# Norm weights folded into the rounding of x, K tile by K tile, in a two-layer encoder trunk on one core

## The chip, the core and the metric

The kernel runs on one core of a Trainium2 chip. TensorE (PE, with its weight loads PEld), VectorE (DVE), ScalarE (ACT), GpSimd (POOL) and SyncE (SP, which issues the DMAs here) each work through a queue of their own in order, and wait for one another by semaphores. The metric is the time of one execution on the device in microseconds; less is better.

## The reference

The trunk has two layers on 256 tokens of width 1024. Each layer is a half-step feed-forward block, a mixer, and a second half-step feed-forward block, and each of the three starts with an RMS norm:

```python
def rmsnorm(x, g):
    x32 = x.astype(jnp.float32)
    y = x32 * lax.rsqrt(jnp.mean(x32 * x32, axis=-1, keepdims=True) + EPS)
    return (y * g.astype(jnp.float32)).astype(x.dtype)
...
    for i in range(DEPTH):
        h = rmsnorm(x, ffn1_norm[i])
        x = x + 0.5 * swiglu(h, ffn1_w_gate[i], ffn1_w_up[i], ffn1_w_down[i])
        h = rmsnorm(x, mix_norm[i])
        proj = h @ w_in[i]
        ...
        x = x + jnp.concatenate([o_s, o_m], axis=-1) @ w_out[i]
        h = rmsnorm(x, ffn2_norm[i])
        x = x + 0.5 * swiglu(h, ffn2_w_gate[i], ffn2_w_up[i], ffn2_w_down[i])
```

`swiglu` is `(silu(h @ w_gate) * (h @ w_up)) @ w_down` with an inner width of 2816. The mixer of layer 0 is chunked attention with a learned bias, that of layer 1 is differential attention with rotary positions; both have four heads of attention into a memory of 256 rows besides. Everything is in 32-bit floats.

## The kernel before, in words

**Products.** Every operand of a product is split into a high part, rounded to the type fp32r, and a low part, the rest. `dense` makes one product of a 128-row K tile: three matmuls into the same PSUM bank, high by high (line 379), high by low of the weights (382), low of x by high of the weights (385), each 128x128 by 128x512.

**Weights.** They come in chunks of 1 MB (`raw`, three buffers, loads in line 270), are rounded by ACT (`hi`, line 300) and DVE (`lo`, line 310) in four quarters of 512 columns, and stay in four pairs of buffers. The chunks of the first feed-forward block are cut in four loads each for the first two chunks; the loads of x are issued between them.

**x.** It lies as two blocks of 128 tokens, each in two halves of 512 columns. `prep_half` turns one half of one token block into the left operand: four transposes on PE into one PSUM bank `xtp` (line 392), a multiply with the norm weight on DVE (`y`, line 423; after the transpose the weight of a column is one value per partition), a cast on ACT (`xh`, line 426), and a subtraction on DVE (`xl`, line 428). A half holds four K tiles; x has eight (`KT`), K tiles 0 to 3 in half 0 and 4 to 7 in half 1. The factor of the row, 1/rms, is applied after the products: `square` sums the squares on ACT (line 437), `prep_rstd` makes `xr` of them.

`prep_half` runs 24 times: four times at the start (`start`), and four times at each of the five entries to the following stages, from `finish`, which adds the accumulated sum to x (lines 462 and 465) half by half.

**Order.** The order on each queue is not written out; a planner sets it while the program is built. `Flow` keeps a clock `now`, advanced by the estimated time of each matmul or transpose, and a time `free` for each other engine. Steps are generators: a `yield` of a time means "not before", a `yield` of a function means "when this holds". Whenever PE's clock moves, steps that are due are issued, those due earliest first; weight rounding (`split_hi`, `split_lo`) is spawned as idle work, issued when nothing else is due. `dense` waits until the planner has its operands: `xt.t[tb][k]` for x and `lot` for the weights. The estimates are

```python
HOP = 0.22
T_MM = 0.216
T_TR = 0.107
...
    def act(self, n, extra=0.0):
        return self.eng("A", 0.15 + n / 1200.0 + extra)
    def dve(self, n, extra=0.0):
        return self.eng("V", 0.07 + n / 960.0 + extra)
```

The start of the kernel is set by hand: the clock begins at 2.7, the four halves of x are due at four written times (line 1308: 3.75 for block 0 half 0, 8.2 for block 0 half 1, 7.4 for block 1 half 0, 10.4 for block 1 half 1), and arrivals of weights are estimated in `loader` from 2.3 on with 2.9 for a chunk and 1.5 of latency. The first feed-forward block takes K tiles 0 to 3 of both token blocks, then 4 to 7 of both.

Of the kernel before, what the change touches and what calls it, by code (L numbers as in the profile page):

```python
# [12 lines left out]
F32 = mybir.dt.float32  # L13
# [3 lines left out]
AF = mybir.ActivationFunctionType  # L17
ALU = mybir.AluOpType
AX = mybir.AxisListType

P = 128
# [121 lines left out]
def kernel(  # L143
# [10 lines left out]
    nc = tc.nc  # L154
    PSUM = bass.MemoryType.PSUM
    NRAW, NHL, NT2 = 3, 4, 19
    flow = Flow()
# [13 lines left out]
    g2 = Slots(flow, t2, "t", NT2)  # L171
# [5 lines left out]
    def bank(name, shape=(P, 4, P)):  # L177
        return banks.take(list(shape), F32, name)
# [36 lines left out]
    gcol = const.tile([P, NGC], F32, name="gcol")  # L215
    gcs = const.tile([P, 4], F32, name="gcs")

    def gain_columns():
        grow = const.tile([NGC - 16, P], F32, name="grow")
        for src, r0 in ((mix_norm, GC_MIX), (mem_norm, GC_MEM), (ffn2_norm, GC_FFN2)):  # L220
            later(grow[r0 - 16:r0, :], src.rearrange("l (k p) -> (l k) p", p=P))
        for src, r0, n in ((mem_q_norm, GC_MQ, 2), (mem_k_norm, GC_MK, 2), (a_q_norm, GC_AQ, 1),
                           (a_k_norm, GC_AK, 1)):
            for j in range(2):
                later(grow[r0 - 16:r0 - 16 + n, j * HD:(j + 1) * HD], src)
        later(grow[GC_SUB - 16:GC_SUB - 15, :], b_subln)
        yield from loaded()
        yield banks.has()
        tp = bank("gps")
        nc.tensor.transpose(out=tp[:, 0, :NGC - 16], in_=grow, identity=ident[:NGC - 16, :NGC - 16])  # L230
        yield flow.pe(T_TR)
        nc.vector.tensor_copy(gcol[:, 16:], tp[:, 0, :NGC - 16])
        banks.give()
        nc.vector.tensor_scalar_mul(gcs[:, 0:2], gcol[:, GC_MQ:GC_MQ + 2], HD ** -0.5)
        nc.vector.tensor_scalar_mul(gcs[:, 2:3], gcol[:, GC_AQ:GC_AQ + 1], HD ** -0.5)
        nc.vector.tensor_scalar_mul(gcs[:, 3:4], gcol[:, GC_SUB:GC_SUB + 1], 1.0 - LAMBDA_INIT)
        flow.dve(0, 0.5)
# [153 lines left out]
    def turn(dst, src, flipped=False):  # L391
        nc.tensor.transpose(out=dst, in_=src, identity=flip if flipped else ident)  # L392
        return flow.pe(T_TR)
# [19 lines left out]
    def prep_half(xt, tb, hf, gc, wait=0.0):  # L413
        yield banks.has()
        tp = bank("xtp")
        for k in range(4):
            t = turn(tp[:, k, :], xs[tb][:, hf * 512 + k * P:hf * 512 + (k + 1) * P])
        yield t
        yield g2.has()
        y = g2.take([P, 4, P], F32, "y")  # L420
        ks = slice(hf * 4, hf * 4 + 4)
        g = gcol[:, gc + hf * 4:gc + hf * 4 + 4]
        nc.vector.tensor_tensor(out=y, in0=tp, in1=g.unsqueeze(2).broadcast_to([P, 4, P]), op=ALU.mult)
        banks.give()
        yield flow.dve(512)
        nc.scalar.copy(out=xt.h[tb][:, ks, :], in_=y)
        yield flow.act(512)
        nc.vector.tensor_sub(xt.l[tb][:, ks, :], y, xt.h[tb].bitcast(F32)[:, ks, :])
        g2.give()
        t = flow.dve(512)  # L430
        for k in range(hf * 4, hf * 4 + 4):
            xt.t[tb][k] = t
        flow.spawn(square(xt, tb, hf, flow.now + wait))

    def square(xt, tb, hf, t):
        yield t
        nc.scalar.activation(junk, xs[tb][:, hf * 512:(hf + 1) * 512], AF.Square,
                             accum_out=xt.ss[tb][:, hf:hf + 1])
        yield flow.act(512, 0.1)
        xt.done[tb] += 1  # L440
        if xt.done[tb] == 2:
            yield from prep_rstd(xt, tb)
# [13 lines left out]
    def finish(acc, tb, xt, gc, half):  # L456
        for hf in range(2):
            sl = slice(hf * 512, (hf + 1) * 512)
            yield lambda: acc.t[tb][hf] is not None
            yield acc.t[tb][hf]  # L460
            if half:
                nc.vector.scalar_tensor_tensor(out=xs[tb][:, sl], in0=acc.ps[tb][hf], scalar=0.5, in1=xs[tb][:, sl],
                                               op0=ALU.mult, op1=ALU.add)
            else:
                nc.vector.tensor_add(xs[tb][:, sl], acc.ps[tb][hf], xs[tb][:, sl])
            banks.give()
            yield flow.dve(512)
            if xt is None:
                nc.sync.dma_start(out=out[0, tb * P:(tb + 1) * P, sl], in_=xs[tb][:, sl])
            else:  # L470
                yield from prep_half(xt, tb, hf, gc)
# [807 lines left out]
    xt = Xt()  # L1279
# [12 lines left out]
    def start(tb, hf, t):  # L1292
        yield t
        yield from prep_half(xt, tb, hf, GC_FFN1, 3.0)
# [10 lines left out]
    flow.spawn(start_gain())  # L1305
    for tb in range(2):
        for hf in range(2):
            flow.spawn(start(tb, hf, (3.75, 8.2, 7.4, 10.4)[2 * tb + hf]))
    flow.spawn(gain_columns())
    flow.spawn(rope_setup(), idle=True)  # L1310
    flow.spawn(lambda_setup())
# [2 lines left out]
    for l in range(DEPTH):  # L1314
        xt = ffn(l, 1, xt, GC_MIX + l * KT)
        xt = mixer(l, xt, GC_FFN2 + l * KT)
        xt = ffn(l, 2, xt, None if l == DEPTH - 1 else GC_FFN1 + (l + 1) * KT)
# [53 lines left out]
```

## Time and profile before

| | |
|---|---|
| median of 3 runs | 970.88 us (970.84 to 972.41) |
| the profiled execution | 970.84 us, span in the profile 969.1 us |
| busy: PE, PEld, DVE, ACT, POOL | 960.4, 788.3, 681.8, 545.7, 60.2 us |
| granted PE clock | 1.00 |
| moved by DMA | 204 MB, 211 GB/s on average |

The span is the time from the first to the last recorded event; what lies around it, 1.7 us, is not in the records. PE counts as busy while a matmul is in flight, and matmuls overlap, so its 99% does not say that it works at its peak; it says that there is hardly a stretch without one.

### The profile page before, as it was taken

To read this page: it belongs to the slowest core of one execution; us is meant where nothing else is said; L and a number is where in the kernel's file an instruction comes from. 1 tells how busy PE (TensorE), PEld (TensorE's weight loads), DVE (VectorE), ACT (ScalarE), POOL (GpSimd) and SP (SyncE) were. 2 spreads that over 40 slices of the span, in tenths; PEclk is the share of its full clock that TensorE was granted. 3 is DMA by queue.
4 is the path that set the end of the run, shared out by engine and by line. 5 is a ranking of instruction groups with operands and counts; after the bars stand their busy time and mean duration, and the time that the engine had idled before them with its cause. 6 is when DMAs were issued, how large, how long until landed. Compare 5 with 4: busy or idle time off the path is not lost.

```text
span 969.1 us, 13332 instructions
## 1 busy us (share of the span) xinstructions
PE 960.4 (99%) x4552; PEld 788.3 (81%) x4552; DVE 681.8 (70%) x1428; ACT 545.7 (56%) x1167; POOL 60.2 (6%) x65
## 2 busy tenths in 40 slices
PE   8999999999999999999999999999999999999998
PEld 7888888888777888888888888888787788888886
DVE  6777777788787877665566666654999986666641
ACT  6665555667675655554455545443677764545440
POOL 0000000021210000000000000000344100000000
PEclk9999999999999999999999999999999999999999
DMA  9988877385525587776648777764641468877741
GB/s 286 323 272 279 262 261 242 128 283 195 175 90 171 182 254 238 237 248 231 197 132 275 245 228 247 239 218 132 211 137 50 139 199 265 252 249 240 236 131 43
DMA packets 169295, 204.03 MB, mean 211 GB/s; under 512 B 9674, under 2 KB 144395, under 8 KB 169227
## 3 DMA queue, kind: packets, MB, share of 16 engines
q1 hardware_dynamic: 169226, 203.18, 65.3%
q8 instruction: 35, 0.57, 0.2%
q14 instruction: 34, 0.27, 0.1%
HBM read 188.99 MB, written 14.16 MB: 210 GB/s over the span
## 4 chain that ended last, share of the span: by engine, by line
PE 93%; DVE 4%; ACT 1%; DMA 1%; SPq 0%; issue 0%; ACTq 0%
PE gu L385 16%; PE gu L382 16%; PE gu L379 16%; PE acc L379 10%; PE acc L385 10%; PE acc L382 10%; PE pj L385 3%; PE pj L382 3%; PE pj L379 3%; DVE lo L310 1%; PE xtp L392 1%; PE S L1012 1%; PE AV L1093 1%; PE ptp L392 1%; PE kv L382 1%; PE kv L385 1%
## 5 line engine op out<-in xcount | busy, mean ns | idle before, releaser
L310 DVE TENSOR_TENSOR lo<-raw,hi 128x512 fp32r<-128x512 f32 x656 | 418.0, 684 | 196.2 <-ACT hi L300 182.6
L300 ACT CAST hi<-raw 128x512 fp32r<-128x512 f32 x656 | 367.0, 618 | 281.0 <-PE gu L385 149.9
L385 PE MATMUL gu<-hi,xl 128*128 128x512 f32 x704 | 274.3, 390 | 0.0
L379 PE MATMUL gu<-hi,xh 128*128 128x512 f32 x704 | 274.1, 389 | 0.0
L382 PE MATMUL gu<-lo,xh 128*128 128x512 f32 x704 | 274.0, 389 | 0.0
L382 PEld LDWEIGHTS gu<-lo,xh 128*128 128x128 f32 x704 | 132.2, 188 | 27.4
L385 PEld LDWEIGHTS gu<-hi,xl 128*128 128x128 f32 x704 | 132.2, 188 | 27.3
L379 PEld LDWEIGHTS gu<-hi,xh 128*128 128x128 f32 x704 | 132.2, 188 | 27.3
L379 PE MATMUL acc<-hi,ht 128*128 128x512 f32 x352 | 137.6, 391 | 0.0
L382 PE MATMUL acc<-lo,ht 128*128 128x512 f32 x352 | 137.2, 390 | 0.0
L385 PE MATMUL acc<-hi,ht 128*128 128x512 f32 x352 | 137.1, 390 | 0.0
L385 PEld LDWEIGHTS acc<-hi,ht 128*128 128x128 f32 x352 | 66.1, 188 | 13.7
L382 PEld LDWEIGHTS acc<-lo,ht 128*128 128x128 f32 x352 | 66.1, 188 | 13.5
L379 PEld LDWEIGHTS acc<-hi,ht 128*128 128x128 f32 x352 | 66.1, 188 | 13.5
L385 PE MATMUL pj<-hi,xl 128*128 128x512 f32 x160 | 64.5, 403 | 0.0
L382 PE MATMUL pj<-lo,xh 128*128 128x512 f32 x160 | 63.6, 397 | 0.0
L379 PE MATMUL pj<-hi,xh 128*128 128x512 f32 x160 | 63.5, 397 | 0.0
L487 ACT ACTIVATE sil<-gu,xr 128x256 f32<-128x256 f32 x88 | 41.4, 471 | 22.6 <-PE gu L385 22.6
L490 DVE SCALAR_TENSOR_TENSOR h<-gu,xr,sil 128x256 f32<-128x256 f32 x88 | 42.3, 480 | 2.3
L399 POOL TENSOR_TENSOR xr<-v,nhalf 128x1 f32<-128x1 f32 x12 | 8.4, 697 | 506.3 <-DVE v L397 506.3
L517 DVE TENSOR_TENSOR ht<-hr,ht 128x512 fp32r<-128x512 f32 x44 | 30.2, 686 | 13.4 <-ACT ht L515 12.9
L498 DVE STREAM_TRANSPOSE hb<-h 128x256 f32<-128x256 f32 x88 | 38.7, 440 | 1.1
(165 smaller groups left out, 828.0 us busy)
## 6 DMA issues: line engine op xcount, KB each, us to landing
raw<-in_ffn_w_down_dram SPq DMA_DIRECT2D x176, 256.0 KB, 4.1
raw<-in_ffn_w_gate_dram SPq DMA_DIRECT2D x86, 512.0 KB, 4.1
raw<-in_ffn_w_up_dram SPq DMA_DIRECT2D x86, 512.0 KB, 5.1
raw<-in_w_in_dram SPq DMA_DIRECT2D x32, 512.0 KB, 4.9
hd<-hb SPq DMA_DIRECT2D x44, 256.0 KB, 2.0
hr<-hd SPq DMA_DIRECT2D x44, 256.0 KB, 5.2
raw<-in_w_out_dram SPq DMA_DIRECT2D x8, 1024.0 KB, 4.9
raw<-in_w_mem_kv_dram SPq DMA_DIRECT2D x4, 1024.0 KB, 5.4
```

Source lines behind the costliest of these rows:

```text
L300: nc.scalar.copy(out=c.hi[:, sl], in_=c.raw[:, sl])
L310: nc.vector.tensor_sub(c.lo[:, sl], c.raw[:, sl], c.hi.bitcast(F32)[:, sl])
L379: nc.tensor.matmul(out=ps, lhsT=xh, rhs=wh, start=start, stop=False)
L382: nc.tensor.matmul(out=ps, lhsT=xh, rhs=wl, start=False, stop=False)
L385: nc.tensor.matmul(out=ps, lhsT=xl, rhs=wh, start=False, stop=stop)
L392: nc.tensor.transpose(out=dst, in_=src, identity=flip if flipped else ident)
L487: nc.scalar.activation(sil, ps[tb][:, 0:256], AF.Silu, scale=xt.r[tb])
L490: nc.vector.scalar_tensor_tensor(out=h, in0=ps[tb][:, 256:512], scalar=xt.r[tb], in1=sil, op0=ALU.mult, op1=ALU.mult)
L498: nc.vector.transpose(out=hb[:, :, tb].rearrange("p b f j -> p f b j"), in_=h.rearrange("p (f b i) -> p f b i", f=2, b=4))
L517: nc.vector.tensor_sub(lo, src, hi.bitcast(F32))
L1012: nc.tensor.matmul(out=ss[e][:, pr, :nk], lhsT=q[rows, pr, :], rhs=k[rows, pr, :], start=i == 0, stop=i == len(passes) - 1)
L1093: nc.tensor.matmul(out=av[64 * e:64 * e + 64, pr, :], lhsT=vsrc(kb, pr, e), rhs=pts[e][:, pr, kb, :], start=(kb == 0), stop=(kb == nb - 1))
```

## The change

The multiply on DVE goes, and so does its buffer `y`. ACT now reads each K tile out of the PSUM bank, multiplies it with its norm weight (one value per partition, as the scale) and rounds it to `xh` in the same instruction, four times 128 columns. DVE reads each K tile out of PSUM too, multiplies it again and subtracts `xh`, four times 128 columns. All four ACT steps are issued together; the DVE steps follow, each when the planner takes its ACT step as done, and each K tile is reported ready to `dense` by itself. The bank is given back after the last DVE step; it was given back after the multiply before. At the start, the written times of the four halves are later by 1.15, 1.1, 1.1 and 0.8 of the planner's us, which puts the first products ahead of the transposes of token block 1 half 0 in PE's queue.

```diff
         yield t
-        yield g2.has()
-        y = g2.take([P, 4, P], F32, "y")
-        ks = slice(hf * 4, hf * 4 + 4)
-        g = gcol[:, gc + hf * 4:gc + hf * 4 + 4]
-        nc.vector.tensor_tensor(out=y, in0=tp, in1=g.unsqueeze(2).broadcast_to([P, 4, P]), op=ALU.mult)
+        ts = []
+        for k in range(4):
+            kk = hf * 4 + k
+            nc.scalar.activation(xt.h[tb][:, kk, :], tp[:, k, :], AF.Copy, scale=gcol[:, gc + kk:gc + kk + 1])
+            ts.append(flow.act(P, 0.02))
+        for k in range(4):
+            kk = hf * 4 + k
+            yield ts[k]
+            nc.vector.scalar_tensor_tensor(out=xt.l[tb][:, kk, :], in0=tp[:, k, :], scalar=gcol[:, gc + kk:gc + kk + 1],
+                                           in1=xt.h[tb].bitcast(F32)[:, kk, :], op0=ALU.mult, op1=ALU.subtract)
+            xt.t[tb][kk] = flow.dve(P, 0.06)
         banks.give()
-        yield flow.dve(512)
-        nc.scalar.copy(out=xt.h[tb][:, ks, :], in_=y)
-        yield flow.act(512)
-        nc.vector.tensor_sub(xt.l[tb][:, ks, :], y, xt.h[tb].bitcast(F32)[:, ks, :])
-        g2.give()
-        t = flow.dve(512)
-        for k in range(hf * 4, hf * 4 + 4):
-            xt.t[tb][k] = t
         flow.spawn(square(xt, tb, hf, flow.now + wait))
...
-            flow.spawn(start(tb, hf, (3.75, 8.2, 7.4, 10.4)[2 * tb + hf]))
+            flow.spawn(start(tb, hf, (4.9, 9.3, 8.5, 11.2)[2 * tb + hf]))
```

## The prediction

> **What bounds the kernel now.** I read the page first, then the busy time by stretches, then the timeline of the start and of the entry to the second mixer.
>
> ```profile
> PE 960.4 (99%) x4552; PEld 788.3 (81%) x4552; DVE 681.8 (70%) x1428; ACT 545.7 (56%) x1167; POOL 60.2 (6%) x65
> ...
> PE 93%; DVE 4%; ACT 1%; DMA 1%; SPq 0%; issue 0%; ACTq 0%
> ```
>
> The first line says that TensorE (PE) is busy 99% of the span; the second, that the chain of work that ended last runs over PE for 93%. The products are a fixed number in a fixed queue, so a change of the norm step can win only where PE stands still. There are two such places: the start, before the first product, and the second mixer.
>
> ```profile
> 668.00:690.00 22.00, 22.00 (x106) 18.18 (x105) 15.94 (x30) 12.83 (x27) 2.08 (x2) 1.00 0.40 137
> 688.00:760.00 72.00, 70.25 (x386) 55.21 (x384) 66.46 (x152) 51.70 (x150) 29.76 (x26) 1.00 0.38 124
> ```
>
> In these lines the columns are the stretch, its length, and busy time (and instructions) of PE, PEld, DVE, ACT, POOL. In 668 to 690, the entry to the second mixer with four of the 24 norm halves, PE is busy 22.00 of 22.00 us while DVE has 15.94 and ACT 12.83: neither is full. In 688 to 760 PE is idle 72 - 70.25 = 1.75 us, and DVE with 66.46 of 72 is the engine it waits for.
>
> The start, in order of time (x of two issues at 3.64 are token block 1 half 0 and block 0 half 1; the one at 5.79 is block 1 half 1):
>
> ```profile
> 1.64 0.43 SPq L270 DMA_DIRECT2D raw<-in_ffn_w_gate_dram  x1
> ...
> 3.13 0.47 SPq L270 DMA_DIRECT2D raw<-in_ffn_w_up_dram  x1
> ...
> 3.64 0.94 SPq L186 DMA_DIRECT2D x<-in_x_dram  x2
> ...
> 5.79 0.47 SPq L186 DMA_DIRECT2D x<-in_x_dram  x1
> ...
> 8.66 0.66 PE L392 MATMUL xtp<-ident,x 128*128 128x128 f32 x4 [1.62 <-DMA x<-in_x_dram]
> ...
> 9.07 0.47 PE L379 MATMUL gu<-hi,xh 128*128 128x512 f32 x1
> ...
> 9.62 0.60 PE L392 MATMUL xtp<-ident,x 128*128 128x128 f32 x4
> ...
> 11.68 0.39 PE L379 MATMUL gu<-hi,xh 128*128 128x512 f32 x1
> ...
> 12.10 0.42 PEld L392 LDWEIGHTS xtp<-ident,x 128*128 128x128 f32 x4 [0.46 <-DMA x<-in_x_dram]
> ...
> 12.52 0.48 PE L382 MATMUL gu<-lo,xh 128*128 128x512 f32 x1
> ...
> 13.06 0.39 PE L379 MATMUL gu<-hi,xh 128*128 128x512 f32 x1
> ...
> 18.05 0.39 PE L382 MATMUL gu<-lo,xh 128*128 128x512 f32 x1
> ```
>
> PE waits 1.62 us for the load of x block 1 half 0, transposes it at 8.66, and only then starts the first product, at 9.07. The other two sets of transposes follow at 9.62 and 12.10. The last set again waits for its load: its first weight load, at 12.10, was 0.46 idle before. From 13.06 to 18.05 lie 22 steps: (18.05 - 13.06) / 22 = 0.227 us for a product (here one matmul of 128x512, three to a K tile). The last transposes before 12.52 are those of block 1 half 1; at that point PE has done 12 transposes of the late halves and ten products: three each for K tiles 0, 1 and 2 and one for K tile 3 (the one at 11.68).
>
> **The norm step, one half.** Prices now, and the nearest ones for what replaces them:
>
> ```profile
> L423 DVE TENSOR_TENSOR y<-xtp,gcol 128x512 f32<-128x512 f32 x24 | 16.5, 689 | 16.7 <-PE xtp L392 16.7
> L428 DVE TENSOR_TENSOR xl<-y,xh 128x512 fp32r<-128x512 f32 x24 | 16.5, 687 | 4.1 <-ACT xh L426 3.9
> ...
> L426 ACT CAST xh<-y 128x512 fp32r<-128x512 f32 x24 | 14.8, 617 | 35.7 <-DVE y L423 35.7
> ...
> L1125 ACT ACTIVATE pe<-S,nm 128x128 f32<-128x128 f32 x12 | 4.3, 367 | 4.9 <-DVE nm L1118 4.9
> ...
> L1099 ACT CAST oT<-AV 128x256 fp32r<-128x256 f32 x10 | 3.7, 372 | 7.3 <-PE AV L1093 7.2
> ...
> L674 ACT ACTIVATE qmT<-qmtp,gcs 128x256 fp32r<-128x256 f32 x4 | 1.9, 484 | 0.9 <-PE qmtp L392 0.9
> ```
>
> ```profile
> L662 DVE SCALAR_TENSOR_TENSOR meml<-mr,gcol,memh 128x128 fp32r<-128x128 f32 x32 | 8.9, 345 | 0.0
> ```
>
> ```profile
> 178.86 1.13 DVE L662 SCALAR_TENSOR_TENSOR meml<-mr,gcol,memh 128x128 fp32r<-128x128 f32 x4
> ```
>
> *Removed:* a multiply on DVE (0.689 us), a cast on ACT (0.617), a subtraction on DVE (0.687). *Added:* four scaled copies of 128x128 on ACT and four scalar_tensor_tensor of 128x128 on DVE.
>
> ACT: no 128-wide scaled copy is in the trace. A 256-wide one from PSUM takes 484 ns against 372 for the plain cast, so the scale column costs about 0.11; a 128-wide activation with a column takes 367 ns (the 128x128 group of L1125, the nearest row). Four back to back: the four casts at 6.93 in the next fence take 2.23, where four times 0.617 is 2.47, so 0.08 overlaps at each of three joints, and 4 x 0.367 - 3 x 0.08 = 1.23 us. The bounds are 0.617 (no more than one cast now) and 4 x 0.484 = 1.94. At 1.23 ACT gets 0.61 more per half, 24 x 0.61 = 14.6 us in all, on an engine that is busy 545.7 of 969.1.
>
> DVE: the same form, out of SBUF, does four in 1.13 us. So a half falls from 1.376 to 1.13, by 0.25, in all 6 us. The bounds: four at the full 0.345 each, 1.38, save nothing; if four cost what the one subtraction costs now, 0.69 is saved. I take 0.25, since L423 (out of PSUM) and L428 (out of SBUF) differ by 2 ns only.
>
> **Where K tile by K tile is lost.** Both engines now read one PSUM bank for one half. The trace shows what the program does with that:
>
> ```profile
> 732.64 0.41 DVE L677 TENSOR_TENSOR k<-qktp,k 128x256 fp32r<-128x256 f32 x1
> ```
>
> ```profile
> 733.09 0.38 ACT L672 CAST q<-qktp 128x256 fp32r<-128x256 f32 x1 [1.72 <-DVE k L677]
> ```
>
> In qktp, DVE rounds the k columns and ACT then casts the q columns, other columns of the same tile. ACT needs nothing that DVE makes, and yet it waits for it 1.72 us and starts 0.04 after its end (732.64 + 0.41 = 733.05). So two readers of one tile in PSUM are kept apart, in the order of issue. The Trainium skill, PSUM — Partial Sum Buffer, section "PSUM bank collisions raise a hardware error", says the same: two engines may not be in one bank at once, reads against reads included, and a scheduler puts a dependency between them; by that rule too, the pipelining is lost and the sum below stays as it is. In the change all four ACT copies are issued before the first DVE step. The first DVE step therefore starts after the fourth copy, and not after the first.
>
> Latency of a half, from its transposes on: before, 5.68 to 7.75, 2.07 us:
>
> ```profile
> 5.68 0.69 DVE L423 TENSOR_TENSOR y<-xtp,gcol 128x512 f32<-128x512 f32 x1 [1.83 <-PE xtp L392]
> 6.41 0.62 ACT L426 CAST xh<-y 128x512 fp32r<-128x512 f32 x1 [4.19 <-DVE y L423]
> ...
> 6.93 2.23 ACT L300 CAST hi<-raw 128x512 fp32r<-128x512 f32 x4
> 7.06 0.69 DVE L428 TENSOR_TENSOR xl<-y,xh 128x512 fp32r<-128x512 f32 x1 [0.68 <-ACT xh L426]
> ...
> 7.67 1.89 DVE L310 TENSOR_TENSOR lo<-raw,hi 128x512 fp32r<-128x512 f32 x3
> ...
> 15.81 1.29 DVE L310 TENSOR_TENSOR lo<-raw,hi 128x512 fp32r<-128x512 f32 x2
> ```
>
> The step from one engine to the next takes 0.04 (6.37 to 6.41). After, 1.23 + 0.04 + 1.13 = 2.40 for the last K tile and 1.23 + 0.04 + 0.345 = 1.62 for the first. If the readers were not kept apart, it would be 1.62 and 0.367 + 0.04 + 0.345 = 0.75. The new wait stands in DVE's queue, for up to 1.23 - 0.367 = 0.86 us per half, and behind it are the roundings lo of weights (L310), which PE needs. What hides it at an entry:
>
> ```profile
> 686.90 0.69 DVE L428 TENSOR_TENSOR xl<-y,xh 128x512 fp32r<-128x512 f32 x1
> ...
> 689.72 1.89 DVE L310 TENSOR_TENSOR lo<-raw,hi 128x512 fp32r<-128x512 f32 x3 [0.48 <-ACT hi L300]
> ```
>
> ```profile
> 683.42 0.60 PE L392 MATMUL xtp<-ident,x 128*128 128x128 f32 x4
> ...
> 689.32 0.39 PE L385 MATMUL pj<-hi,xl 128*128 128x512 f32 x1
> ```
>
> The last half of that entry is transposed at 683.42; its xl ends at 686.90 + 0.69 = 687.59, and the first product with it is at 689.32: 1.73 us of cover against 2.40 - 2.07 = 0.33. DVE also stands idle 0.48 us just behind, at 689.72. So the five entries (20 halves) cost PE nothing; without that cover, each would cost up to 0.33. A bank is held until the last DVE step, 2.40 instead of the 0.69 of y, 1.7 us longer; with PE busy 22.00 of 22.00 no wait for a bank is there to be made longer. I cost that at nothing; the bound is one wait of 1.7.
>
> **The start, step by step.** The order on each queue comes from the planner's own clock in the source, so I follow it. Before: transposes of block 0 half 0 at 3.75, ready 4.40; y at 5.22; the cast is issued at 5.22, just ahead of the first weight cast hi at 5.25. The first product is due at 7.45, and the transposes of block 1 half 0, due 7.4, go ahead of it: that is the order at 8.66. After: transposes at 4.9 are ready at 5.55; now hi quarters 0 and 1 (due 5.25) go *ahead* of the four copies on ACT. Copies end at 6.76 to 7.59; DVE has lo 0, lo 1, then xl 0, due 7.81. The first product is due at 7.81, ahead of 8.5. Its three products end at 8.46; one of K tile 1 follows (8.67), then the transposes of block 1 half 0 (8.5 is past), one product (9.32), the transposes of block 0 half 1 (9.3), and the rest of K tiles 1, 2 and 3 up to 11.26. Only then, with 11.2 past, come those of block 1 half 1.
>
> On the chip: the first weight quarter lands between these two:
>
> ```profile
> raw<-in_ffn_w_gate_dram SPq DMA_DIRECT2D x1, 256.0 KB, 3.0
> ```
>
> ```profile
> raw<-in_ffn_w_up_dram SPq DMA_DIRECT2D x1, 256.0 KB, 4.8
> ```
>
> Issued at 1.64 and 3.13, they land at 4.6 and 7.9; three pieces further in 3.3 us is 1.1 a piece, so the piece that hi 0 needs is in at about 5.7 (an estimate; at the latest 6.93, where hi 0 ran without waiting). Then on ACT hi 0 and 1 end at 6.8, the copies at about 7.9, and xl 0 at 8.3. PE starts its first product near 7.1 and has three or four done when x block 1 half 0 lands at 8.66. After that: two sets of transposes at 0.44 each and eight more products, 8.66 + 0.88 + 8 x 0.227 = 11.4, where it waits for x block 1 half 1. That load is the same as now, so those transposes still run at 12.10 and the next product at about 12.52. By then 12 products are done instead of ten: 2 x 0.227 = **0.45 us gained**, and a first product 2 us earlier brings no more. There are 0.7 us of spare time in front of 12.10; a landing of hi 0 later than 6.4 would eat into the gain, at 6.93 it is about all gone (0.5 late).
>
> Is the gain kept? DVE finishes the last two lo quarters of the second chunk at 15.81 + 1.29 = 17.10; the product that needs the last one runs at 18.05, so 0.95 of slack, of which 0.45 is used. ACT has 4 x 0.61 = 2.4 us more to do:
>
> ```profile
> 9.00:13.00 4.00, 3.96 (x23) 3.09 (x22) 3.16 (x6) 2.96 (x7) 0.00 (x0) 1.00 1.06 365
> 13.00:20.00 7.00, 7.00 (x32) 5.78 (x32) 6.55 (x14) 5.76 (x15) 0.55 (x1) 1.00 1.07 326
> ```
>
> In these two stretches it is free for (4.00 - 2.96) + (7.00 - 5.76) = 2.28 us, and it starts 0.7 us earlier than 6.41. So the gain is kept, barely.
>
> Sum: 970.84 (the profiled execution; its span is 969.1, the 1.74 around it stay) - 0.45 + 0 (entries) = **970.4**. The runs' median, 970.88, is 0.04 above that execution.
>
> **Rivals.** *No gain at all* (970.84): hi 0 lands late, or lo quarters of the second chunk come 0.5 us late behind the added ACT work. Chance 0.12. *Faster, the second mixer moves up*: the relief of 0.25 per half on DVE and the earlier K tiles let DVE enter its full stretch earlier, or the planner's new order there happens to fit better; at most PE's idle 1.75 us is won, 970.84 - 0.45 - 1.75 = 968.6. For it: DVE is what PE waits for from 689.72 on. Against: DVE idles 0.48 just there, waiting for ACT, so earlier work is not passed on. Chance 0.20. *Slower, DVE held by ACT*: the 0.86 us wait at the head of each half comes on top, with no DVE saving out of PSUM, and four halves lead into the DVE-bound stretch: 4 x 0.86 - 0.48 = 2.96 us late at 689.72, 970.84 - 0.45 + 2.96 = 973.4. It decides from the point where DVE comes to 689.72 more than 0.48 late with no second pause to absorb it. The Trainium skill's rule on banks is what makes this wait; the trace agrees by the 1.72 us above. Against: DVE has 22.00 - 15.94 = 6.06 us free in 668 to 690, and the waits mostly fall where it would have waited for the cast anyway. Chance 0.18. The forecast keeps 0.50.
>
> **How the numbers follow.** What a measurement of this kernel can tell from no change is about 0.2%, 1.9 us. Forecast and first rival lie inside that, 0.62; the second rival gives 0.21 for faster with a little of the forecast's tail, the third 0.17 for slower. The forecast alone goes from 970.0 to 970.9. The range reaches to most of both other cases, 968.5 to 973.2, leaving out some 0.18.
>
> **What would show it.** Right: two groups of four on ACT and DVE for each half, near 0.37 and 0.35 each; the first DVE step behind the fourth copy; first product near 7 to 8 us; 12 products ahead of the transposes at 12.1; the product that was at 18.05 at 17.6; PE full in 668 to 690. Wrong: PE waiting for lo between 15 and 18 us, DVE reaching the stretch at 689.72 late, or another order of the second mixer's queues, seen as PE idle far from 1.75 us.

## The result, and the profile after

The kernel after takes 974.06 us (median of 11 runs, 972.86 to 975.58), the kernel before 971.02 in the same comparison (11 runs, 970.84 to 972.41): the ratio is 1.0027, 95% interval 1.0018 to 1.0035. So it is slower by 0.27%, where 970.4 was forecast, and above the upper end of the forecast range, 973.2. The profiled execution took 973.49 us, 2.65 more than the one of before. From its page, busy time and the chain that ended last:

```profile
PE 962.4 (99%) x4552; PEld 788.4 (81%) x4552; DVE 676.9 (70%) x1476; ACT 556.0 (57%) x1239; POOL 61.9 (6%) x65
...
PE 92%; DVE 4%; ACT 2%; DMA 1%; issue 0%; SPq 0%; ACTq 0%; DVEq 0%
```

DVE lost 4.9 us of work and ACT gained 10.3, as intended, and PE still runs through the whole span. The two new groups (busy, mean ns of one, then idle time ahead of them and what ended it):

```profile
L422 ACT ACTIVATE xh<-xtp,gcol 128x128 fp32r<-128x128 f32 x96 | 27.2, 369 | 26.7 <-PE xtp L392 26.7
L427 DVE SCALAR_TENSOR_TENSOR xl<-xtp,gcol,xh 128x128 fp32r<-128x128 f32 x96 | 27.1, 344 | 21.4 <-ACT xh L422 21.2
```

The prices of single steps were right: 369 ns against 367 for a copy, 344 against 345 for a DVE step. The start, in order of time:

```profile
6.42 1.14 ACT L300 CAST hi<-raw 128x512 fp32r<-128x512 f32 x2 [4.20 <-DMA raw<-in_ffn_w_up_dram]
...
7.46 1.13 ACT L422 ACTIVATE xh<-xtp,gcol 128x128 fp32r<-128x128 f32 x4
...
7.87 0.50 PE L379 MATMUL gu<-hi,xh 128*128 128x512 f32 x1 [0.65 <-ACT xh L422]
...
8.62 1.13 DVE L427 SCALAR_TENSOR_TENSOR xl<-xtp,gcol,xh 128x128 fp32r<-128x128 f32 x4 [0.27 <-ACT xh L422]
...
12.33 0.60 PE L392 MATMUL xtp<-ident,x 128*128 128x128 f32 x4
...
17.80 0.50 PE L382 MATMUL gu<-lo,xh 128*128 128x512 f32 x1 [0.22 <-DVE lo L310]
...
18.62 0.41 PE L382 MATMUL gu<-lo,xh 128*128 128x512 f32 x1
```

The first product comes at 7.87, and 12 products are done when the transposes at 12.33 run, as worked out. But at 17.80 PE waits for `lo`, and the product that was at 18.05 is at 18.62: 0.57 late, and not early.

How the 2.65 us lie along the span is read by following one product through both traces, since their number and order is the same. Product 40 (counted from 0) is at 19.41 in before, 2830 at 685.69 (entry to the second mixer), 3300 at 820.89 (behind it). The table has the increments of that product's delay against before's trace, and the spans (before: 969.1), in us, from one profiled execution of each kernel; the last four are the experiments below:

| kernel | up to product 40 | then to 2830 (holds the first mixer) | then to 3300 (the second mixer) | delay at 3300 | span |
|---|---|---|---|---|---|
| after | 0.61 | 0.15 | 1.88 | 2.64 | 971.7 |
| fold at the five entries only | -0.03 | 0.14 | 1.88 | 1.99 | 971.2 |
| fold at the start only | 0.09 | -0.01 | 0.02 | 0.10 | 969.2 |
| new instructions, old order | -0.06 | -0.01 | 0.30 | 0.23 | 969.3 |
| old instructions, new order | 0.62 | 0.18 | 2.44 | 3.24 | 972.3 |

The delay at product 3300 is the difference of the spans within 0.1. Of after's 2.64 two thirds lie in the second mixer, and a quarter at the start. In 690.5 to 787 before has 94.75 us of PE busy and 541 matmuls:

```profile
690.50:787.00 96.50, 94.75 (x541) 75.17 (x540) 87.41 (x191) 67.29 (x187) 28.80 (x26) 1.00 0.44 142
```

After has 22.00 of 22.00 still at the entry, but less PE time in the second stretch, and eight matmuls fewer done in it:

```profile
668.00:690.00 22.00, 22.00 (x106) 18.22 (x105) 14.92 (x38) 14.07 (x38) 2.33 (x3) 1.00 0.35 116
690.50:787.00 96.50, 93.93 (x533) 73.92 (x532) 85.66 (x190) 66.09 (x190) 30.34 (x26) 1.00 0.44 135
```

What is different there is the order of PE's queue. The dense products follow each other as before, but the other matmuls stand elsewhere among them: compared place by place, by the names of their tiles, 462 of PE's 4552 matmuls are others, nearly all in 180 to 340 us and in 660 to 800, which hold the two mixers. Before, the four `AV` products go straight into the twelve `S` products:

```profile
707.88 0.60 PE L1150 MATMUL AV<-V,PT 128*128 128x128 f32 x4
708.42 0.97 PE L1012 MATMUL S<-k,q 64*128 64x256 f32 x12
709.32 0.50 PE L379 MATMUL pj<-hi,xh 128*128 128x512 f32 x1
```

After, three products of the projection `pj` stand between:

```profile
707.61 0.60 PE L1148 MATMUL AV<-V,PT 128*128 128x128 f32 x4
707.97 0.48 PE L385 MATMUL pj<-hi,xl 128*128 128x512 f32 x1
708.28 0.40 PE L379 MATMUL pj<-hi,xh 128*128 128x512 f32 x1
708.52 0.40 PE L382 MATMUL pj<-lo,xh 128*128 128x512 f32 x1
708.85 0.97 PE L1010 MATMUL S<-k,q 64*128 64x256 f32 x12
```

### The profile page after: what moved, and what is told of

Its sections match the earlier page's. It is cut to its first block, busy times and chain, and to the rows that moved or that the text cites. A ratio compares the mean times of both kernels' runs of the same rounds, so it can differ in the third digit from the quotient of the medians.

```text
span 971.7 us, 13468 instructions
## 1 busy us (share of the span) xinstructions
PE 962.4 (99%) x4552; PEld 788.4 (81%) x4552; DVE 676.9 (70%) x1476; ACT 556.0 (57%) x1239; POOL 61.9 (6%) x65
## 4 chain that ended last, share of the span: by engine, by line
PE 92%; DVE 4%; ACT 2%; DMA 1%; issue 0%; SPq 0%; ACTq 0%; DVEq 0%
PE gu L385 16%; PE gu L382 16%; PE gu L379 16%; PE acc L385 10%; PE acc L382 10%; PE acc L379 10%; PE pj L385 3%; PE pj L379 3%; PE pj L382 3%; DVE lo L310 1%; PE S L1010 1%; PE xtp L392 1%; PE AV L1091 1%; PE ptp L392 1%; PE kv L379 1%; PE kv L385 1%
## 5 line engine op out<-in xcount | busy, mean ns | idle before, releaser
L513 ACT CAST ht<-hr 128x512 fp32r<-128x512 f32 x44 | 27.1, 615 | 42.6 <-DMA hr<-hd 42.4
L422 ACT ACTIVATE xh<-xtp,gcol 128x128 fp32r<-128x128 f32 x96 | 27.2, 369 | 26.7 <-PE xtp L392 26.7
```

The lines of the kernel that those rows point to most:

```text
L422: nc.scalar.activation(xt.h[tb][:, kk, :], tp[:, k, :], AF.Copy, scale=gcol[:, gc + kk:gc + kk + 1])
L513: nc.scalar.copy(out=hi, in_=src)
```

## The experiments

**Fold at the entries only** (the old steps and times at the start) and **fold at the start only** (the old steps at the entries):

```diff
# prep_old: the three instructions of before; prep_new: the eight of after
# entries only                                  # start only
 def finish:  yield from prep_new(xt, tb, hf, gc)   def finish:  yield from prep_old(...)
 def start:   yield from prep_old(...)              def start:   yield from prep_new(...)
 times (3.75, 8.2, 7.4, 10.4)                       times (4.9, 9.3, 8.5, 11.2)
```

> Fold at the five entries only; the start has the old norm step and the old times. In the changed kernel the products were 0.6 us late after the start, 0.85 late in front of the second mixer and 2.75 late behind it. If these parts stand by themselves: no delay until 180 us, 0.2 in front of the second mixer, about 2.1 at the end (973.0). If the loss in the second mixer comes from arriving there late after a bad start: under 0.5 in all (971.4).

> Fold and new times at the start only; the entries have the old norm step. If the parts stand by themselves: 0.6 us late from 20 us on and still so at the end (971.6), mixers as before. If the loss in the second mixer is a consequence of the late start: about 2.5 late (973.5). The prediction's step for the start: 0.45 us early (970.5).

Entries only: 974.21 us, ratio 1.0029 (1.0017 to 1.0041), all of the loss, of which the trace shows 1.99 us. Start only: 971.53, ratio 0.9998 (0.9990 to 1.0007), nothing lost and nothing won, where 0.6 us late or 0.45 early was expected. So the loss comes from the five entries. That the start was 0.61 late in after's profile does not come back in the start-only kernel (0.09), whose first quarter of weights was rounded earlier (first `hi` at 5.73 against 6.42). The landing is not the only thing that makes a start late, though: the old instructions in the new order, below, are 0.62 late there with the first `hi` at 5.73 too.

At the entries two things changed together: the instructions, and what the planner is told about their times. **New instructions in the old order** issues the new eight where the old three stood, with the old estimates and with the bank and the slot of `y` given back as before, so that PE's, SP's and POOL's queues are those of before. **Old instructions in the new order** does the opposite; its queues are those of after.

```diff
 # new instructions, old order (against after; start times as before)
-        yield ts[k] ... flow.dve(P, 0.06)
+        yield flow.dve(512)
+        for kk in range(hf * 4, hf * 4 + 4):
+            nc.scalar.activation(...)              # the four scaled copies
+        yield flow.act(512)
+        for kk in range(hf * 4, hf * 4 + 4):
+            nc.vector.scalar_tensor_tensor(...)    # the four DVE steps
 # old instructions, new order (against before; start times as after)
+        for k in range(4):
+            if k == 0: nc.vector.tensor_tensor(out=y, ...); nc.scalar.copy(...)
+            ts.append(flow.act(P, 0.02))
+        for k in range(4):
+            yield ts[k]
+            if k == 0: nc.vector.tensor_sub(...)
+            xt.t[tb][kk] = flow.dve(P, 0.06)
```

> The new instructions (four scaled copies on ACT, four steps on DVE) everywhere, but with the planner told of the old steps, so that PE's, SyncE's and GpSimd's queues are those of before, instruction for instruction, and the four copies stand where the cast stood. Theory ORDER (the loss in the second mixer is the new order of the queues): within 0.3 us of before in the second mixer. Theory HELD (DVE stands behind ACT's four copies, the third rival of the prediction): 1.5 to 3 us later there.

> The old three instructions everywhere, but with the planner told of the new steps and times, so that PE's, SyncE's and GpSimd's queues are those of the changed kernel, instruction for instruction. Theory ORDER: the second mixer loses 1.5 to 2.2 us as in the changed kernel, 973 in all. Theory HELD: the second mixer loses under 0.3 us.

The new instructions in the old order: 971.52, ratio 1.0006 (0.9997 to 1.0014). The old ones in the new order: 974.67 (5 runs), ratio 1.0033 (1.0020 to 1.0046), with 2.44 lost in the second mixer, a little more than was expected. The same stretch of the second mixer, entries only, then new instructions in the old order, then old instructions in the new order:

```profile
690.50:787.00 96.50, 93.75 (x532) 74.04 (x532) 85.52 (x193) 66.14 (x192) 29.77 (x25) 1.00 0.42 133
```

```profile
690.50:787.00 96.50, 94.62 (x541) 75.20 (x540) 85.68 (x194) 67.95 (x192) 28.76 (x26) 1.00 0.44 142
```

```profile
690.50:787.00 96.50, 93.55 (x532) 73.57 (x530) 86.62 (x187) 64.00 (x182) 30.39 (x26) 1.00 0.43 136
```

The order decides, not the instructions: where the queues are old (before, the second of these), PE has 541 matmuls done and stands idle 1.75 and 1.88 us; where they are new (after and the other two), 533, 532 and 532, idle 2.57, 2.75 and 2.95. This also answers the rival of DVE held by ACT, as far as the mixer goes. With the new instructions in the old order, the group of DVE steps is

```profile
L427 DVE SCALAR_TENSOR_TENSOR xl<-xtp,gcol,xh 128x128 fp32r<-128x128 f32 x96 | 27.0, 343 | 21.2 <-ACT xh L424 21.2
```

and has the new wait, 21.2 us behind the copies, as in after; yet the second mixer costs 0.30. Before, DVE stood idle for 16.7 and 4.1 us ahead of its two norm steps, 20.8 together, so the new wait stands mostly where others were. What the rival does cost is seen in one place, behind the mixer, at the entry to the last feed-forward block, in this kernel:

```profile
788.22 1.12 DVE L427 SCALAR_TENSOR_TENSOR xl<-xtp,gcol,xh 128x128 fp32r<-128x128 f32 x4 [0.83 <-ACT xh L424]
...
789.26 0.68 DVE L465 TENSOR_TENSOR x<-acc,x 128x512 f32<-128x512 f32 x1
...
789.99 0.42 PEld L392 LDWEIGHTS xtp<-ident,x 128*128 128x128 f32 x4 [0.48 <-DVE x L465]
```

DVE waits 0.83 us for the copies, so it adds the sum to x at 789.26, where before did it at 787.84, and PE's next transposes wait for that. They lie between products 3164 and 3165, and there 0.28 of the 0.30 arises; up to there this kernel is not late at all.

**Only an estimate.** If the order decides, then kernels that differ in nothing but a number that the planner is told must spread too. Three, with the set of instructions unchanged. In the second, the edit reaches only the first of the two DVE steps, the multiply; the estimate of the subtraction stays, unlike what the expectation for that run says:

```diff
 # before, estimate of the cast +0.53       # before, estimate of the multiply on DVE +0.3
-        yield flow.act(512)                -        yield flow.dve(512)
+        yield flow.act(512, 0.53)          +        yield flow.dve(512, 0.3)
 # after, estimate of one DVE step 0.03 longer
-            xt.t[tb][kk] = flow.dve(P, 0.06)
+            xt.t[tb][kk] = flow.dve(P, 0.09)
```

> The kernel before, instruction for instruction the same set; only the planner's estimate for the cast in the norm step is 0.53 of its us longer (as long as the four copies). Theory ORDER: the queues of the mixers change as much as in the changed kernel, and the time moves by 1 us or more either way, with everything outside the mixers within 0.2. Theory FOLD (only the new instructions or their bank use can cost): within 0.5 us of before.

> The kernel before with the same set of instructions; only the planner's estimate for the two DVE steps of the norm step is 0.3 longer each. Theory ORDER: another order of the mixers, the time moves by 1 us or more either way, and by another amount than with the longer estimate for the cast. Theory FOLD: within 0.5 us of before.

> The changed kernel, the same set of instructions; only the planner's estimate for the four DVE steps is 0.03 longer each, which gives a third order of the mixers. Theory ORDER: the second mixer's loss is not the 1.9 us of the changed kernel but another one, between a gain of 1 and a loss of 3. Theory FOLD: 1.9 us again, within 0.3.

The queues do change: by the same comparison, 582 places of PE's queue against before, 260 against before, and 386 against after. The cast's estimate: 972.72, ratio 1.0016 (1.0007 to 1.0025), lost in the first mixer (1.55 us between products 40 and 2830) and not in the second (0.15). The multiply's estimate: 972.17, 1.0009 (1.0000 to 1.0019), with the two mixers together 0.19 us faster than before and the start 2.70 late in the profile. Here the expected 1 us or more was missed: a new order can also cost next to nothing. The step of after: 973.06, 1.0015 (1.0005 to 1.0025), with 1.40 in the second mixer instead of 1.88 and the start 3.73 late. So by one estimate alone the two mixers of before move between 0.19 us faster and 1.70 slower. What the late starts of the last two consist of is told in the last section.

**Squares later at the start.** In the start-only kernel the rounding of the second chunk, then the two squares ahead of the next roundings, and the product that had to wait:

```profile
12.49 1.14 ACT L444 ACTIVATE xh<-xtp,gcol 128x128 fp32r<-128x128 f32 x4
...
13.51 1.16 ACT L300 CAST hi<-raw 128x512 fp32r<-128x512 f32 x2
13.67 1.13 DVE L449 SCALAR_TENSOR_TENSOR xl<-xtp,gcol,xh 128x128 fp32r<-128x128 f32 x4 [0.77 <-ACT xh L444]
...
14.54 0.66 ACT L457 ACTIVATE junk<-x 128x512 bf16<-128x512 f32 x1
...
15.32 0.63 ACT L457 ACTIVATE junk<-x 128x512 bf16<-128x512 f32 x1
...
15.95 1.65 ACT L300 CAST hi<-raw 128x512 fp32r<-128x512 f32 x3
...
16.58 1.89 DVE L310 TENSOR_TENSOR lo<-raw,hi 128x512 fp32r<-128x512 f32 x3 [0.17 <-ACT hi L300]
...
17.33 0.50 PE L382 MATMUL gu<-lo,xh 128*128 128x512 f32 x1 [0.23 <-DVE lo L310]
...
18.13 0.40 PE L382 MATMUL gu<-lo,xh 128*128 128x512 f32 x1
```

ACT has two squares (`junk`, 14.54 to 15.95) ahead of the last three `hi`; DVE's `lo` follows at 16.58, and PE waits for it at 17.33. The next kernel holds the squares of the start back to 15.0 on the planner's clock:

```diff
-        yield from prep_new(xt, tb, hf, GC_FFN1, 3.0)
+        yield from prep_new(xt, tb, hf, GC_FFN1, 15.0)   # square: not before max(flow.now, 15.0)
```

> As the run with the fold and the new times at the start only, with one more edit: the four sums of squares of the start are not issued before 15.0 on the planner's clock, so that on ACT they stand behind all four roundings of the second weight chunk instead of among them. Theory START (products are 0.8 us early up to K tile 3 and lose it because ACT rounds the second chunk's quarters late, behind copies and squares): still 0.4 to 0.8 us early at 20 us and at the end, about 0.5 under before. Rival (the loss is the load of the second chunk, or DVE's): no change from the run without this edit, within 0.1 of before.

```profile
12.44 1.14 ACT L444 ACTIVATE xh<-xtp,gcol 128x128 fp32r<-128x128 f32 x4 [0.30 <-PE xtp L392]
...
13.45 1.68 ACT L300 CAST hi<-raw 128x512 fp32r<-128x512 f32 x3
...
14.65 1.89 DVE L310 TENSOR_TENSOR lo<-raw,hi 128x512 fp32r<-128x512 f32 x3
...
17.25 0.39 PE L382 MATMUL gu<-lo,xh 128*128 128x512 f32 x1
```

`hi` runs right behind the copies, `lo` at 14.65, and the same product is at 17.25 instead of 18.13: 0.80 ahead of before, and this lasts to the end (a span of 968.3 against 969.1). Over the runs it is 970.99 against 971.33, ratio 0.9992 (0.9981 to 1.0002): what the trace shows at the start is not told from no change by the times.

**The last half later still.** PE's weight load still stood 0.45 us for x block 1 half 1 at 11.74. This kernel, on top of the last, sets its time to 12.6 instead of 11.2:

```diff
-            flow.spawn(start(tb, hf, (4.9, 9.3, 8.5, 11.2)[2 * tb + hf]))
+            flow.spawn(start(tb, hf, (4.9, 9.3, 8.5, 12.6)[2 * tb + hf]))
```

> As the run with the squares later, and the last half of x (block 1 half 1) due at 12.6 instead of 11.2 on the planner's clock, so that its transposes stand seven matmuls further back in PE's queue and its four copies behind all four roundings of the second chunk. If PE's wait for the load of that half at 12.1 is what caps the start: 0.5 us more, 1.2 to 1.4 early at the end, about 970.0. If the second chunk of weights comes next: no more than 0.8 early, as before this edit.

The hoped-for gain did not come, and the number of the second expectation, no more than 0.8, held: 971.45, ratio 0.9992 (0.9979 to 1.0005), and 0.54 early at product 34 of the profile instead of 0.80 (0.20 at product 3300). The wait for that load is gone, but the load before it is late instead:

```profile
9.96 0.42 PEld L392 LDWEIGHTS xtp<-ident,x 128*128 128x128 f32 x4 [0.35 <-DMA x<-in_x_dram]
```

The first `hi` also ran 0.27 later than in the kernel with the squares moved (5.90 against 5.63). So in this execution the loads ahead of that half, and not its place in the queue, set the start.

**Two banks.** The start-only kernel with K tiles 0 and 1 in one bank and 2 and 3 in another, with the queues unchanged, executed once:

```diff
-        tp = bank("xtp")
+        tps = [bank("xtp") for _ in range(2)]      # K tile k is read from tps[k // 2]
```

> As the run with the fold and the new times at the start only, with the same order on every queue, but K tiles 0 and 1 of a half are transposed into one PSUM bank and 2 and 3 into another. Theory BANK (readers of one bank are kept apart): the first DVE step of a half starts behind the second copy on ACT, not behind the fourth, about 0.5 us earlier where DVE is free. Rival (DVE waits for the fourth copy for another reason, the order of issue): still behind the fourth.

```profile
13.13 1.14 ACT L444 ACTIVATE xh<-xtp,gcol 128x128 fp32r<-128x128 f32 x4
...
13.79 1.12 DVE L449 SCALAR_TENSOR_TENSOR xl<-xtp,gcol,xh 128x128 fp32r<-128x128 f32 x4 [0.51 <-ACT xh L444]
```

Of the same half in the start-only kernel, the copies begin at 12.49 and the DVE steps at 13.67, 1.18 behind, when the fourth copy is done. With two banks it is 0.66, when the second is. So in this program two readers of one bank are kept apart, and DVE waits until ACT is done with the whole bank. Each bank holds one tile `xtp` here, so whether it goes by the bank or by the tile is not told apart. The one time, 971.54 us, with the first `hi` only at 7.03, doesn't say what that is worth.

## Why the prediction was wrong

**"So the five entries (20 halves) cost PE nothing", the "+ 0 (entries)" of the sum: the step that failed.** As far as the instructions go it nearly held: PE is 22.00 of 22.00 at the entry to the second mixer, and with the old order the whole fold costs 0.23 us in the profile, all of it at the last entry. But the sum took the queues beyond the start as they were; "a fixed number in a fixed queue" holds for the products among themselves, and not for what stands between them. The new yields and estimates go through the planner's clock at all five entries, and the orders of both mixers come out otherwise: 0.15 + 1.88 us. The prediction followed that clock by hand for the start and not for the rest, and let "the planner's new order there happens to fit better" in only on the side of a gain, at most 1.75. It should have stood on the side of a loss too. Its own sign of being wrong, "PE idle far from 1.75 us", is what came: PE is idle 2.57 in that stretch. This accounts for 0.82 of the second mixer's loss. Three of the waits, with no like in before, come to 1.01 us: 0.36 at 757.43 for DVE's `of`, 0.28 at 759.73 and 0.37 at 761.01 for ACT's `pe`; other waits became shorter. The rest of the loss lies in stretches where a matmul is always in flight, and what in the new order costs it stays open. Which of the planner's inputs makes the order, of those that changed at the entries, is told by the queues alone, without a time: with the bank given back early, with the slot of `y` still taken, or with both, they come out as in after, so it is the estimates and yields of the ACT and DVE steps.

**"So the gain is kept, barely": failed too.** The advance was there: product 12 is 0.85 early in the start-only kernel and 0.38 in after, against 0.45 forecast. But the free time of ACT was added up over 9 to 20 us, and not followed in its queue: two squares and four copies stand ahead of the roundings that PE needs, and 0.85 early becomes 0.09 late. With the squares behind them it keeps 0.80. PE waiting for `lo` between 15 and 18 us was named as a sign of being wrong, and it came, at 17.80. In after the first `hi` ran at 6.42, at the edge that the prediction gave for its landing (6.4), so ACT did not start "0.7 us earlier" either.

**"Slower, DVE held by ACT", 973.4.** The number is near the result by luck, for the reason is another. DVE does wait 21.2 us for the copies, in after and in the old order alike, and in the old order PE loses by it not 2.96 us but 0.28, behind the mixer. The premise, that the readers of one tile in PSUM are kept apart, was right, by 1.18 against 0.66 us with two banks. The Trainium skill, PSUM — Partial Sum Buffer, section "PSUM bank collisions raise a hardware error", says that a scheduler keeps two engines apart in one bank, reads against reads included. These runs agree as far as they go: they show the order kept, not what happens without it.

**Right:** the order of the start product by product; four copies in 1.13 us and four DVE steps in 1.13 (forecast 1.23 and 1.13); the first DVE step behind the fourth copy, at 8.62 after 7.46 + 1.13. By the busy time of the instructions themselves, DVE saves 16.5 + 16.5 - 27.1 = 5.9 us (forecast 6) and ACT gets 27.2 - 14.8 = 12.4 more (forecast 14.6): the copies are cheaper as a group. The engines' whole busy times moved by less, 4.9 and 10.3, because the overlap with neighbours and the busy time of other instructions changed too.

**A version that beats both?** The fold at the start alone with the squares moved is the best of them by its trace, at 0.9992 (0.9981 to 1.0002) against before, and ahead of after, whose interval against the same kernel is 1.0018 to 1.0035. That it is ahead of before is seen in one trace, 0.8 us at the start, and not shown by the times.

## What to carry to other kernels

Where a planner or a list scheduler sets the queues, a change of what one step costs or of when it yields changes the order of stages far away; price the new order as a loss too, and compare the queues before the busy times. The idle of those stages gives the order of magnitude alone: it was 1.75 us here, and new orders cost between -0.33 us and 2.44 us in that mixer. To tell the instructions from the order, run each with the other's order. And the free time of an engine over a stretch hides an added step only if that time lies ahead of the instruction that is waited for: follow the queue.

## What was not expected of the hardware

The first loads land at different times from one execution to the next, while they are issued at the same times to 0.01 us up to 3.64: the first `hi` ran at 5.63, 5.73, 5.90, 6.42 and 7.03 us in five profiled executions. In two other profiled executions more was late. In before with the longer estimate of the multiply it was x; in after with the longer DVE step it was the next weights and x:

```profile
9.83 0.66 PE L392 MATMUL xtp<-ident,x 128*128 128x128 f32 x4 [1.81 <-DMA x<-in_x_dram]
```

```profile
10.44 1.14 ACT L300 CAST hi<-raw 128x512 fp32r<-128x512 f32 x2 [2.00 <-DMA raw<-in_ffn_w_up_dram]
...
11.10 0.66 PE L392 MATMUL xtp<-ident,x 128*128 128x128 f32 x4 [1.49 <-DMA x<-in_x_dram]
```

There x block 1 half 0, for which PE waited until 8.66 in before, comes at 9.83 and 11.10. In both executions the granted PE clock then fell to half for a while; in all the others it was 1.00 there. In 12 to 14 us (the clock is the third number from the end; PE did 12 matmuls there in before, at 1.00):

```profile
12.00:14.00 2.00, 2.00 (x6) 1.52 (x6) 1.62 (x3) 1.77 (x5) 0.00 (x0) 0.50 1.10 351
```

```profile
12.00:14.00 2.00, 2.00 (x9) 1.71 (x7) 1.41 (x5) 2.00 (x9) 0.00 (x0) 0.50 1.09 346
```

The trace has it at 0.50 for 3.4 us in each, so 1.7 us of PE's work is lost by the clock (an estimate, 3.4 x 0.5). With the later load, 9.83 - 8.66 = 1.17, that is 2.87 for the first, whose start is 2.70 late. In the second the same transposes stand at 9.60 in after, so the load takes 1.50, together 3.20, and its start is 3.73 - 0.61 = 3.12 later than after's. By this estimate the clock makes more than half of the 2.70 and of the 3.12, and the load the rest. Whether the long wait brings the low clock on is not shown: with the new instructions in the old order PE waited 1.73 us at that place, nearly as long as the 1.81 of the first, and kept 1.00. The two executions took 973.73 and 975.99 us, above the medians of their kernels, 972.17 and 973.06. A single profile of the start can thus be off by more than the whole effect under study.
